# A hybrid encoder layer: block products for part of five input column groups, and one running account for the background work

## The chip, the cores and the metric

The kernel runs on one core of a Trainium2 chip. The metric is the device time of one execution in microseconds (us), the median of several runs. A profiled execution of the same program gives the trace from which all durations below are taken. Engines are named as in the profile: PE multiplies matrices, DVE (vector) and ACT (scalar) do elementwise work, SP issues the DMA transfers. Each engine works through its own instructions in the order in which the program issued them, and waits there for data or for a free buffer.

## The reference

One layer, with 256 positions and 4096 channels, in float32:

```python
xn = rms_norm(x, norm_g[l])
h = jnp.einsum('bsd,de->bse', xn, w_in[l])                # 4096 -> 14336 columns
c_val, c_glu, c_gate, q, k, v, a_gate = jnp.split(h, split_pts, axis=-1)

conv_out = conformer_conv(c_val, c_glu, conv_w[l], ...)   # GLU, depthwise conv of 31 taps,
conv_out = conv_out * jax.nn.silu(c_gate)                 # LayerNorm over channels, swish

q = rms_norm(q.reshape(B, S, ATTN_HEADS, HEAD_DIM), q_norm_g[l])
k = rms_norm(k.reshape(B, S, ATTN_HEADS, HEAD_DIM), k_norm_g[l])
attn = longnet_mixture(q, k, v, rel_bias)                 # 16 heads of 128
attn_out = attn * jax.nn.silu(a_gate)

mixed = jnp.concatenate([conv_out, attn_out], axis=-1)
x = x + jnp.einsum('bse,ed->bsd', mixed, w_out[l])        # 4096 -> 4096
```

The LayerNorm takes its mean and variance over all 2048 convolution channels, so nothing behind it can begin before the last channel is convolved.

## The kernel before

**Matrix products.** To keep float32 precision, every operand is split in two parts, a rounded high part and the rest (`wh`, `wl` for weights, `xh`, `xl` for rows of x), and each product is three matmuls: high by high, low by high, high by low. A matmul takes 128 channels of the contraction, 128 positions and 512 columns. The contraction of 4096 is 32 slices `k`, or 16 pairs of slices; one DMA of 1 MB brings the weights of a pair, 1024 columns wide (`load_pair`). A slice costs 12 matmuls: two halves `e` of the columns, two halves `s` of the positions, three each.

**Groups.** The columns are worked through in 18 groups of 1024 (`GROUPS`): groups 0 to 3 `conv` (value and GLU gate of 512 channels each), then four times `agv` (attention gate and v of four heads) and `qk` (query and key of the same heads), that is 4 to 11, then 12 and 13 `gate` (gates of the convolution), and 14 to 17 `out`. The main loop (from L905 on) issues, for each slice n of the 14 input groups, its first half's high matmuls, the rest of the slice before, the split of the weights three slices ahead (`split_w`, L199: ACT makes `wh`, DVE makes `wl`; eight slots), its first half's low matmuls, and then calls `pump`. At the end of a group `evacuate` (L610) moves the sums out of PSUM, with the factor `rstd` of the normalization of x, which the operands don't hold yet (x is multiplied by `norm_g` alone), and starts the background work that they make possible.

**Background work** is written as generators that issue a few instructions and yield their cost, a pair (DVE ns, ACT ns). `glu_post`, `ag_post` and `gate_post` transpose a tile of 512 channels to channels by positions (`turn`, L299: two DVE transpositions of 32x32 blocks, then four steps of four ACT copies). `conv_gen` (L326) applies the 31 taps to 16 chunks of 128 channels, one DVE instruction a tap and chunk. `ln_gen` (L378) is the LayerNorm. `qk_norm` (L428) normalizes and turns the queries and keys of four heads, `head_gen` (L459) is the attention of one head, with four matmuls of its own. `mix_split_gen` (L528) splits the finished rows for the output groups.

**Lanes.** The generators stand in lanes. `pump` (L588), called once per slice, first fills two accounts, DVE's and ACT's, by a quota (`STEP`, 950 and 1400; in the gate groups `GATE_STEP`, 1300 and 1600) but not above the quota, and then lets the lanes step in a fixed order: the gate lane, the foreground lane `fg` (transpositions, norms and heads in the order in which they came; the first three take one step each), twice the mix lane, and up to eight times the convolution lane. A step takes its cost from the accounts, and no generator steps while one of the two is at or below zero:

```python
        for gen in list(self.gens)[: self.width]:
            if min(left) <= 0:
                break
```

**The output groups** are issued by the class `Out` (L672). Ten of the 16 pairs are plain. Six, the pairs 0 to 5 of attention rows (`FUSED`), are taken as a two by two block product with seven instead of eight block multiplications (21 matmuls instead of 24), which needs sums of blocks of the rows (`mix_fuse`) and of the weights (`split_fused`, L722), four more PSUM banks (`m1`, `m5`, `m6`, `m7`) and further additions at the end (`add_more`, L874). The eight PSUM banks are two sets of four, `acc` and `side`; heads and the LayerNorm use `side`. Weights are split ahead whenever the slots allow it. `OUT_ORDERS` says in which order the pairs come: pairs 8 to 15 are convolution rows, 0 to 7 attention rows, and the first output group begins with 8, 9, 10. Before a pair the code loops until its rows have been issued:

```python
            for k in (2 * j, 2 * j + 1):
                while k not in mh:
                    pump()
```

Of the kernel before, what the change touches and what calls it, by code (L numbers as in the profile page):

```python
# [50 lines left out]
FUSED = (0, 1, 2, 3, 4, 5)  # L51
OUT_ORDERS = [(8, 9, 10, 0, 6, 1, 11, 2, 7, 3, 12, 4, 13, 5, 14, 15)]
OUT_ORDERS += 3 * [(8, 9, 0, 10, 1, 11, 2, 6, 3, 7, 4, 12, 5, 13, 14, 15)]
# [29 lines left out]
class Lane:  # L83
# [9 lines left out]
    def step(self, left):  # L93

        spent = 0
        for gen in list(self.gens)[: self.width]:
            if min(left) <= 0:
                break
            try:
                cost = next(gen) or 0  # L100
            except StopIteration:
                self.gens.remove(gen)
                continue
            cost = cost if isinstance(cost, tuple) else (cost, 0)
            for i in range(2):
                left[i] -= cost[i]
            spent += sum(cost)
        return spent
# [3 lines left out]
def layer_kernel(  # L112
# [17 lines left out]
    def t4(name):  # L130
        return sb.tile([P, 4, 256], F32, tag="c4", bufs=15, name=name)
# [13 lines left out]
    def rsqrt(src, shape, mul, eps, name):  # L145
# [6 lines left out]
        cost = 60 + n  # L152
# [24 lines left out]

    raw_tiles = {}

    def load_pair(j, cuts=(0, 2048), between=None):  # L180

        g, jj = divmod(j, n_pairs)
        if g >= NG:
            return
        if groups[g][0] == "out":
            jj = (OUT_ORDERS[g - n_in][jj] + n_pairs // 2) % n_pairs
# [7 lines left out]
    w_split = {}  # L194

    def ws(name):
        return sb.tile([P, 1024], F32R, tag="ws", bufs=W_SLOTS, name=name)

    def split_w(n):  # L199
        j, kk = divmod(n, 2)  # L200
        src = raw_tiles[j][:, kk]
        wh, wl = ws(f"wh{n}"), ws(f"wl{n}")
        if n:
            nc.scalar.copy(wh, src)  # L204
            nc.vector.tensor_sub(wl, src, wh.bitcast(F32))  # L205
        else:
            a, b = slice(0, 512), slice(512, 1024)
            nc.vector.tensor_copy(wh[:, a], src[:, a])
            split_x(0)
            nc.scalar.copy(wh[:, b], src[:, b])  # L210
            for c in (a, b):
                nc.vector.tensor_sub(wl[:, c], src[:, c], wh[:, c].bitcast(F32))
        w_split[n] = (wh, wl)
        if kk == 1:
            del raw_tiles[j]
            load_pair(j + RAW)

    xh, xl = {}, {}
# [30 lines left out]
    def split_x(k):  # L249
# [6 lines left out]
        xh[k], xl[k] = h, l  # L256

    state = {}

    def finish_rstd():  # L260
# [5 lines left out]
        state["rstd"] = [keep[:, s : s + 1] for s in range(2)]  # L266

# [31 lines left out]
    def turn(tile_, name, flip=False):  # L299
# [6 lines left out]
        for s in range(2):  # L306
            nc.vector.transpose(flat[:, 512 * s : 512 * s + 512], src[:, 512 * s : 512 * s + 512])
            yield 620
        blocks = flat.rearrange("p (s t b x) -> p s t b x", s=2, t=4, b=4)
        dst = src.rearrange("p (t s a x) -> p s t a x", t=4, s=2, a=4)  # L310
        for b in range(4):
# [6 lines left out]
            yield 0, 1240  # L318
# [7 lines left out]
    def conv_gen(cb):  # L326
# [4 lines left out]
        for tp in range(0, 4, 2):  # L331
            for t in (tp, tp + 1):
# [5 lines left out]
                yield 335  # L338
            for k in range(TAPS):
# [4 lines left out]
                for t in (tp, tp + 1):  # L344
# [5 lines left out]
                    yield 335  # L350
# [4 lines left out]
    def channel_mean(srcs, name):  # L355

        tot = sb.tile([P, S], F32, tag="rs_big", bufs=6, name=name + "tot")
        for i, make in enumerate(srcs):
# [6 lines left out]
            yield 1135  # L365
            if i:
                nc.vector.tensor_add(tot, tot, part)
                yield 335
# [9 lines left out]
    def ln_gen():  # L378
# [4 lines left out]
        for cb in range(4):  # L383
            nc.vector.tensor_sub(cT[cb], cT[cb], bcast4(mu))
            yield 1135

        def square(cb):
            sq = t4(f"sq{cb}")
            nc.scalar.activation(sq, cT[cb], AF.Square)
# [4 lines left out]
        for cb in range(4):  # L394
            nc.vector.tensor_mul(cT[cb], cT[cb], bcast4(r))
            yield 1135
        for cb in range(4):
            for t in range(4):
# [5 lines left out]
                if t % 2 == 1:  # L404
                    yield 900
# [4 lines left out]
    def gate_post(cb, g):  # L410
# [4 lines left out]
        for t in range(4):  # L415
            nc.vector.tensor_mul(cT[cb][:, t, :], cT[cb][:, t, :], g[:, t, :])
            mix_ready[NH + 4 * cb + t] = cT[cb][:, t, :]
            yield 335
# [9 lines left out]
    def qk_norm(hg):  # L428
        st = sb.tile([P, 16], F32, tag="rs_small", bufs=6, name=f"ssqk{hg}")
        both = (qt[hg], kt[hg])  # L430
        for i, src in enumerate(both):
            sq = t4(f"sq{hg}_{i}")
            nc.scalar.activation(sq, src, AF.Square)
            yield 0, 1000
            yield
            for s in range(2):
# [5 lines left out]
                yield 600  # L442
        r = yield from rsqrt(st, [P, 16], 1.0 / DH, NORM_EPS, f"rqk{hg}")
        for i, src in enumerate(both):
            for s in range(2):
# [5 lines left out]
                yield 600  # L451
# [4 lines left out]
        yield 650  # L456
        qk_ready[hg] = True

    def head_gen(hg, hh):  # L459
        h = 4 * hg + hh  # L460
        hs = slice(DH * hh, DH * hh + DH)
        while hg not in qk_ready:
# [24 lines left out]
        yield 1200  # L487
# [5 lines left out]
        yield 0, 700  # L493
# [3 lines left out]
        yield 600  # L497
        tmp = t2(f"turn_p{h}")
        nc.vector.transpose(tmp, pr)  # L499
        yield 620  # L500
        blocks = tmp.rearrange("p (i j b x) -> p j i b x", i=2, j=2, b=4)
        dst = pr.rearrange("p (j i a x) -> p j i a x", j=2, i=2, a=4)
        for b in range(4):
# [5 lines left out]
            yield 0, 800  # L509
# [11 lines left out]
        yield 400  # L521
# [6 lines left out]
    def mix_split_gen():  # L528
        waiting, done = list(OUT_ORDERS[0]), 0
        while waiting:  # L530
# [10 lines left out]
            if j in FUSED:  # L541
                yield from mix_fuse(j)
                continue
            for kk in (2 * j, 2 * j + 1):
# [5 lines left out]
                yield 335  # L550

    def mix_fuse(j):


        a0, a1 = mix_ready[2 * j], mix_ready[2 * j + 1]
        a11, a21, a12, a22 = a0[:, :P], a0[:, P:], a1[:, :P], a1[:, P:]
        sums = t2(f"mix_sums{j}")
        s1, s2, s3, s4 = (sums[:, P * i : P * i + P] for i in range(4))
        nc.vector.tensor_add(s1, a21, a22)
        nc.vector.tensor_sub(s2, s1, a11)  # L560
        yield 400
        nc.vector.tensor_sub(s3, a11, a21)
        nc.vector.tensor_sub(s4, a12, s2)
        yield 400
        b0, b1 = new_split(2 * j, "m"), new_split(2 * j + 1, "m")
        more = sb.tile([P, 2, 512], F32R, tag="c4", bufs=15, name=f"mx{j}")
        parts = [[b[:, :P] for b in b0], [b[:, P:] for b in b0], b1]
        parts.append([more[:, i, : 3 * P] for i in range(2)])
        for (h, l), src in zip(parts, (a11, s1, a1, sums[:, P:])):
            nc.scalar.copy(h, src)  # L570
            nc.vector.tensor_sub(l, src, h.bitcast(F32))
            yield 300, 300
        names = {"a11": parts[0], "s1": parts[1]}
        names["a12"] = [b[:, :P] for b in b1]
        names["a22"] = [b[:, P:] for b in b1]
        for i in range(3):
            names[f"s{i + 2}"] = [more[:, hl, P * i : P * i + P] for hl in range(2)]
        mx[j] = names
# [7 lines left out]
    left = [0, 0]  # L586

    def pump():  # L588

        for i, quota in enumerate(GATE_STEP if progress["in"] >= 0 else STEP):  # L590
# [417 lines left out]
```

## Time and profile before

| | us |
|---|---|
| median of the three runs | 1602.81 |
| lowest and highest run | 1602.33, 1603.76 |
| the profiled execution | 1603.12 |
| span of its trace, first to last instruction | 1601.3 |
| PE busy in the span | 1590.5 |
| DVE busy | 1195.0 |
| ACT busy | 968.2 |

The mean granted clock of PE is 0.998 of full speed. In the rows below a line of the groups view reads: source line, engine, operation, result and operands, shapes, count; then busy time, mean duration of one in ns; then the idle time of the engine before them and what ended it. A line of the view of one source line gives the shortest, median and longest duration in ns and the start of the first and last in us. Lines of the views in time begin with start and duration. A busy share of PE alone does not say that it works at its peak; the distance from one matmul's start to the next does.

### The profile page before, as it was taken

Reading aid. Unit: us, or ns where it says so; the run is one execution under the profiler, and the core shown is the slowest. Engines: PE = TensorE matmul, PEld = TensorE weight load, DVE = VectorE, ACT = ScalarE, POOL = GpSimd, SP = SyncE. Lnnn points to the kernel's source line nnn. Section 1 sums busy time; section 2 is a strip of 40 time slices with the busy share of each in tenths; the row PEclk is TensorE's granted clock in tenths of the full one; section 3 lists DMA queues with packets and bytes.
Section 4 is the critical chain, followed back from the end, with each engine's and each line's share of the span. In section 5 each row is a group of like instructions: output and inputs, shape, how many; then the busy total and the mean of one; then the engine's idle time right before and its main releaser. Section 6 shows DMA issues by size and latency. Waiting matters only on the chain.

```text
span 1601.3 us, 18984 instructions
## 1 busy us (share of the span) xinstructions
PE 1590.5 (99%) x6986; PEld 1312.8 (82%) x6986; DVE 1195.0 (75%) x1630; ACT 968.2 (60%) x1480; POOL 0.2 (0%) x4
## 2 busy tenths in 40 slices
PE   9999999999999999999999999999999999999999
PEld 7888888888888888888888888888878877888887
DVE  6668888888888887678755556555467889888886
ACT  6763534445453467755779557754789865545453
POOL 0000000000000000000000000000000000000000
PEclk9999999999999999999999999999999999999999
DMA  9755555555555555555555555455545556665653
GB/s 377 289 184 198 196 186 201 192 184 207 188 190 204 184 195 191 186 186 191 179 195 189 192 203 190 173 187 207 194 163 190 184 210 232 232 229 215 248 198 143
DMA packets 52892, 323.53 MB, mean 202 GB/s; under 512 B 5792, under 2 KB 8480, under 8 KB 16192
## 3 DMA queue, kind: packets, MB, share of 16 engines
q1 hardware_dynamic: 52512, 322.05, 56.4%
q8 instruction: 54, 0.88, 0.2%
q10 hardware_dynamic: 288, 0.28, 0.1%
q14 instruction: 38, 0.31, 0.1%
HBM read 318.08 MB, written 4.23 MB: 201 GB/s over the span
## 4 chain that ended last, share of the span: by engine, by line
PE 96%; ACT 1%; DVE 1%; issue 0%; DMA 0%; DVEq 0%; ACTq 0%
PE acc L662 25%; PE acc L663 25%; PE acc L665 25%; PE c L784 5%; PE c L782 5%; PE c L783 5%; PE m L784 1%; PE m L782 1%; PE m L783 1%; PE po L514 1%; PE psc L475 1%; ACT gate L315 0%; ACT pr L505 0%; DMA first_x<-in_x_cols_dram 0%; DVE t24l L736 0%
## 5 line engine op out<-in xcount | busy, mean ns | idle before, releaser
L205 DVE TENSOR_TENSOR wl<-raw,wh 128x1024 fp32r<-128x1024 f32 x447 | 546.9, 1224 | 336.9 <-ACT wh L204 335.9
L204 ACT CAST wh<-raw 128x1024 fp32r<-128x1024 f32 x447 | 469.6, 1052 | 434.9 <-PE acc L663 241.5
L662 PE MATMUL acc<-wh,xh 128*128 128x512 f32 x1792 | 703.8, 393 | 1.3 <-ACT xh L252 1.3
L663 PE MATMUL acc<-wh,xl 128*128 128x512 f32 x1792 | 698.4, 390 | 0.0
L665 PE MATMUL acc<-wl,xh 128*128 128x512 f32 x1792 | 483.7, 389 | 0.0
L662 PEld LDWEIGHTS acc<-wh,xh 128*128 128x128 f32 x1792 | 337.0, 188 | 72.3 <-ACT xh L252 1.6
L663 PEld LDWEIGHTS acc<-wh,xl 128*128 128x128 f32 x1792 | 336.8, 188 | 70.1 <-DVE xl L253 0.2
L665 PEld LDWEIGHTS acc<-wl,xh 128*128 128x128 f32 x1792 | 336.3, 188 | 70.3
L346 DVE SCALAR_TENSOR_TENSOR cT<-conv,wT,cT 128x241 f32<-128x241 f32 (+14 forms) x480 | 201.6, 471 | 0.0
L782 PE MATMUL c<-oh,mh 128*128 128x512 f32 x320 | 125.3, 391 | 0.5 <-ACT oh L716 0.5
L784 PE MATMUL c<-ol,mh 128*128 128x512 f32 x320 | 125.1, 391 | 0.5 <-DVE ol L717 0.5
L783 PE MATMUL c<-oh,ml 128*128 128x512 f32 x320 | 125.0, 391 | 0.0
L716 ACT CAST oh<-raw 128x1024 fp32r<-128x1024 f32 x80 | 83.2, 1051 | 50.8 <-PE c L783 34.4
L717 DVE TENSOR_TENSOR ol<-raw,oh 128x1024 fp32r<-128x1024 f32 x80 | 96.1, 1222 | 21.8 <-ACT oh L716 15.2
L505 ACT COPY pr<-turn_p 32x128 f32<-32x128 f32 x256 | 75.9, 297 | 9.2 <-DVE turn_p L499 5.7
L782 PEld LDWEIGHTS c<-oh,mh 128*128 128x128 f32 x320 | 60.5, 189 | 13.5 <-ACT oh L716 1.0
L784 PEld LDWEIGHTS c<-ol,mh 128*128 128x128 f32 x320 | 60.3, 189 | 13.5 <-DVE ol L717 1.0
L783 PEld LDWEIGHTS c<-oh,ml 128*128 128x128 f32 x320 | 60.5, 189 | 12.8
L732 ACT CAST t24h<-t 128x1024 fp32r<-128x1024 f32 x24 | 25.2, 1051 | 40.3 <-PE c L783 24.1
L736 DVE TENSOR_TENSOR t24l<-t,t24h 128x1024 fp32r<-128x1024 f32 x24 | 29.4, 1226 | 17.3 <-ACT t24h L732 17.3
L732 ACT CAST t13h<-t 128x1024 fp32r<-128x1024 f32 x24 | 25.3, 1053 | 18.2 <-DVE t L748 14.2
L732 ACT CAST bh<-raw 128x1024 fp32r<-128x1024 f32 x24 | 25.3, 1053 | 16.3 <-PE m L783 16.3
(195 smaller groups left out, 1030.8 us busy)
## 6 DMA issues: line engine op xcount, KB each, us to landing
raw<-in_w_dram SPq DMA_DIRECT2D x286, 1024.0 KB, 4.8
x<-in_x_dram SPq DMA_DIRECT2D x8, 512.0 KB, 7.4
xr<-in_x_dram SPq DMA_DIRECT2D x8, 512.0 KB, 6.0
out_dram<-xr SPq DMA_DIRECT2D x15, 256.0 KB, 2.9
xT<-in_x_cols_dram SPq DMA_DIRECT2D x7, 512.0 KB, 6.9
T<-bias_dram SPq DMA_DIRECT2D x16, 192.0 KB, 5.0
raw<-in_w_dram SPq DMA_DIRECT2D x3, 512.0 KB, 6.2
raw<-in_w_dram SPq DMA_DIRECT2D x2, 256.0 KB, 4.4
```

What stands on the lines that cost most here:

```text
L204: nc.scalar.copy(wh, src)
L205: nc.vector.tensor_sub(wl, src, wh.bitcast(F32))
L346: nc.vector.scalar_tensor_tensor(c[:, t, lo:hi], a[:, t, lo + sh : hi + sh], wT[:, ch, k : k + 1], c[:, t, lo:hi], op0=ALU.mult, op1=ALU.add,)
L505: nc.scalar.copy(dst[32 * b : 32 * b + 32, :, :, 3 - a, :], backwards(blocks[32 * a : 32 * a + 32, :, :, b, :]),)
L662: nc.tensor.matmul(a, hs, wp, start=k == 0, stop=False)
L663: nc.tensor.matmul(a, ls, wp, start=False, stop=False)
L665: nc.tensor.matmul(a, hs, wp, start=False, stop=k == KT - 1)
L716: nc.scalar.copy(h, src)
L717: nc.vector.tensor_sub(l, src, h.bitcast(F32))
L782: nc.tensor.matmul(acc, a[0], b[0], start=start, stop=False)
L783: nc.tensor.matmul(acc, a[1], b[0], start=False, stop=False)
L784: nc.tensor.matmul(acc, a[0], b[1], start=False, stop=stop)
```

## The change

1. **Block products in the input.** Groups 2 to 6 (the third to the seventh) take pairs 2, 4, 6 and 8 as seven block products, the other twelve as before. They are issued by the class that was `Out`, now `Stream`, which also splits the weights of all groups. These groups use both sets of PSUM banks, so heads wait for group 7 (`state["side"]`).
2. **Normalized x.** Block sums mix positions, so `rstd` can't be applied at the end: during group 1 x is loaded a second time, multiplied by `norm_g` and `rstd` (laid out along the positions by way of DRAM) and split again (`split_xn`); the sums of the four pairs are made there too. From group 2 on `evacuate` has no factor.
3. **The account.** The quotas are gone. Every matmul that is issued credits both accounts with a share of its time (`FILL`), up to `SAVED`; splits, evacuations and background steps all spend from them, at costs that are set anew.
4. **Others.** The first output group has four block pairs, not six; the block sums use other signs, are made in place in the weights' buffer, and the rows of block pairs are also split as plain ones; the residual x is loaded two pairs earlier; the big tiles (`c4`) have 18 buffers instead of 15, for which a DMA scratch area is cut to 2048 bytes; 11 instead of 7 warm-up matmuls.

```diff
-STEP, GATE_STEP = (950, 1400), (1300, 1600)
-AHEAD = 3
+PRODUCT = 227
+FILL, SAVED = (0.93, 0.93), (1300, 1600)
 RAW = 3
+C4 = 18
...
+FUSED_IN = range(2, 7)
+FUSED = [(2, 4, 6, 8) if g in FUSED_IN else () for g in range(N_IN)] + [range(4)] + 3 * [range(6)]
+ORDERS = N_IN * [range(16)]
+ORDERS += [(8, 9, 10, 0, 6, 1, 11, 2, 7, 3, 12, 4, 13, 5, 14, 15)]
...
+    left = [0, 0]
+
+    def spend(dve, act=0):
+        left[0] -= dve
+        left[1] -= act
+
+    def credit(ns):
+        for i in range(2):
+            left[i] = min(left[i] + FILL[i] * ns, SAVED[i])
...
+    def split_xn(k):
+        src = xT[k]
+        nc.vector.scalar_tensor_tensor(
+            src, src, g_cols[:, k : k + 1], state["rstd_row"], op0=ALU.mult, op1=ALU.mult
+        )
+        h, l = new_split(k, "n")
+        nc.scalar.copy(h, src)
+        nc.vector.tensor_sub(l, src, h.bitcast(F32))
+        xh[k], xl[k] = h, l
+        spend(900, 400)
...
     def turn(tile_, name, flip=False):
...
-            yield 620
+            yield 700
...
-            yield 0, 1240
+            yield 0, 1610
...
     def conv_gen(cb):
...
-                    yield 335
+                    yield 470
...
     def head_gen(hg, hh):
...
-        while hg not in qk_ready:
+        while hg not in qk_ready or not state["side"]:
             yield
...
-        yield 1200
+        yield 1370
...
-        yield 0, 700
+        yield 0, 1380
...
-        yield 600
+        yield 860
...
-        yield 620
+        yield 700
...
-            yield 0, 800
+            yield 0, 1190
...
-    def pump():
-        for i, quota in enumerate(GATE_STEP if progress["in"] >= 0 else STEP):
-            left[i] = min(left[i] + quota, quota)
-        gate_lane.step(left)
-        fg.step(left)
+    def pump(more=0):
+        credit(more)
+        gate_lane.step(left, spend)
+        fg.step(left, spend)
         for _ in range(2):
-            mix_lane.step(left)
+            mix_lane.step(left, spend)
         for _ in range(8):
-            if not conv_lane.step(left):
+            if not conv_lane.step(left, spend):
                 break
...
     def products(n, e, part):
...
+        credit(PRODUCT * (4 - 2 * part))
...
     class Stream:
...
             def part(k):
...
                 nc.scalar.copy(h, src)
                 nc.vector.tensor_sub(l, src, h.bitcast(F32))
+                spend(1225, 1055)
...
             def three():
                 r = blocks()
                 hl = halves("b22s", "b22")
                 nc.scalar.copy(hl[:, 0, :], r[:, 3, :])
+                nc.vector.tensor_add(r[:, 0, :], r[:, 0, :], r[:, 3, :])
+                nc.vector.tensor_add(r[:, 1, :], r[:, 0, :], r[:, 2, :])
+                nc.vector.tensor_sub(hl[:, 1, :], r[:, 3, :], hl[:, 0, :].bitcast(F32))
+                spend(2050, 620)
...
         def triple(self, acc, a, b, start, stop):
...
+            credit(3 * PRODUCT)
...
                 for k in (2 * j, 2 * j + 1):
+                    while k not in rows[0]:
+                        pump(PRODUCT)
...
-    for _ in range(7):
+    for _ in range(11):
         nc.tensor.matmul(spin[:, :P], ones, ones, start=True, stop=True)
...
+    for g in range(n_in):
+        if FUSED[g]:
+            stream.group(g)
+            continue
+        if g > FUSED_IN[-1]:
+            state["side"] = True
+        for k in range(KT):
...
                 products(n, 0, 0)
                 if k == KT - 1:
                     products(n, 0, 1)
                 if k > 0 and n > 1:
                     products(n - 1, 1, 0)
                     products(n - 1, 1, 1)
                 if n + 3 < KT:
                     split_x(n + 3)
+                stream.step()
                 if k < KT - 1:
                     products(n, 0, 1)
...
+            if g == FUSED_IN[0] - 1:
+                if k % 4 == 0:
+                    load_xT(k, 4, nc.sync)
+                if k >= 2:
+                    split_xn(k - 2)
...
             pump()
```

More of the change, by code (lines that the diff above doesn't have):

```diff
@@ L192, in load_pair @@
                 between()
[L194 to L218, printed above, removed]
+    xh, xl, xsum = {}, {}, {}
     def new_split(k, nm):
@@ L832, in fused @@
             )
-            for i, (acc, an, bn, freed) in enumerate(rows):
+            for i, (acc, an, bn, freed) in enumerate(order):
                 self.before()
@@ L840, in fused, with plain @@
                     pump()
[L842 to L858 removed]
+        def plain(self, u, j, rows, one, first):
             for k in range(2):
@@ L948, in layer_kernel @@
     progress["in"] = KT + 2
-    out.run()
+    for g in range(n_in, NG):
+        stream.group(g)
 def _layout(i):
```

455 lines of the change are left out of this document (254 added, 201 removed).

## The prediction

> **What bounds the kernel now.** I read the page's first part, the waits of PE, the groups of instructions, and then single rows in time.
>
> ```profile
> span 1601.3 us, 18984 instructions
> PE 1590.5 (99%) x6986; PEld 1312.8 (82%) x6986; DVE 1195.0 (75%) x1630; ACT 968.2 (60%) x1480; POOL 0.2 (0%) x4
> ...
> 9.29 0.93 PE acc L665 x4
> 13.40 0.91 PE acc L665 x4
> 16.12 0.91 PE acc L665 x4
> ...
> PE m L782 <- ACT t24h L732: 1.2, 1, 1.2
> PE m L784 <- DVE t24l L736: 1.1, 3, 0.5
> ```
>
> The matmul stream sets the time. One slice k (12 matmuls) takes 16.12 - 13.40 = 2.72 us, 0.2267 us a matmul, and PE hardly waits: the two waits shown are the longest that the 24 block-product pairs of the output groups cause (some 3 us over all of them). So matmuls removed count in full, as long as DVE and ACT deliver what PE reads, and that includes the background work: convolution, LayerNorm, attention, gates. When is it done today?
>
> ```profile
> L346 DVE SCALAR_TENSOR_TENSOR cT<-conv,wT,cT x480: 430/471/482, 114.4 to 697.4; 128x242 f32<-128x242 f32 x16, 128x245 f32<-128x245 f32 x16, 128x248 f32<-128x248 f32 x16, 128x251 f32<-128x251 f32 x16
> L400 ACT ACTIVATE cT<-cT,vec_cols x16: 584/595/610, 800.8 to 868.3; 128x256 f32<-128x256 f32 x16
> L519 DVE TENSOR_TENSOR agv<-agv,po x16: 382/414/417, 648.0 to 1245.0; 128x256 f32<-128x256 f32 x16
> L782 PE MATMUL c<-oh,mh x320: 387/389/628, 1257.8 to 1596.5; 128*128 128x512 f32 x160
> ```
>
> Convolution taps end at 697 us, LayerNorm at 868, the last head at 1245; the output groups begin at 1257.8. The heads end 13 us before they are needed; the convolution has long been done.
>
> **The change, part by part.**
>
> *Matmuls.* A plain pair is 24 matmuls, seven block products are 21. Groups 2 to 6 get 4 such pairs each: 5 x 4 x 3 = 60 fewer. The first output group goes from six to four: 6 more. Net -54 x 0.2267 = **-12.2 us**.
>
> *Start.* Eleven warm-up matmuls instead of seven.
>
> ```profile
> 1.04 3.36 PE L900 MATMUL spin<-ones 128*128 128x128 f32 x14 [1.04 <-DVE ones L143]
> 5.73 0.80 PE L662 MATMUL acc<-wh,xh 128*128 128x512 f32 x1 [1.33 <-ACT xh L252]
> 6.85 0.63 PE L662 MATMUL acc<-wh,xh 128*128 128x512 f32 x1
> 7.70 0.63 PE L662 MATMUL acc<-wh,xh 128*128 128x512 f32 x1
> ...
> 9.26 1.05 ACT L204 CAST wh<-raw 128x1024 fp32r<-128x1024 f32 x1 [0.47 <-DMA raw<-in_w_dram]
> 11.42 0.39 PE L662 MATMUL acc<-wh,xh 128*128 128x512 f32 x1
> ```
>
> Seven end at 4.40, so 0.48 us each; eleven would end at 6.3, 0.6 us late. In return the first eight real matmuls, 0.42 us apart (two in 7.70 - 6.85), might run at 0.23: at most 8 x 0.2 = 1.6 us back, of which the copy of the third weight slice, ready near 10.3 us where PE used it at 11.4, lets 1.1 through. Between +0.6 and -1.1 I take **-0.5**. The Trainium skill ("TensorE: Matmul & The Clock Gate", section "Part 1: The HAM clock gate") says that the array runs at half rate until a window of about 3.4 us was busy; by that rule a gapless row of warm-up matmuls gives the whole -1.1, and a long idle stretch later costs the slow start again.
>
> *Splitting a block pair.*
>
> ```profile
> L736 DVE TENSOR_TENSOR bl<-raw,bh 128x1024 fp32r<-128x1024 f32 x24 | 29.3, 1221 | 0.5 <-ACT bh L732 0.2
> L748 DVE TENSOR_TENSOR t<-raw 128x1024 f32<-128x1024 f32 x24 | 29.2, 1219 | 0.0
> L759 DVE TENSOR_TENSOR t<-raw,t 128x512 f32<-128x512 f32 x24 | 16.4, 684 | 0.0
> L205 DVE TENSOR_TENSOR wl<-raw,wh 128x1024 fp32r<-128x1024 f32 x447 | 546.9, 1224 | 336.9 <-ACT wh L204 335.9
> L204 ACT CAST wh<-raw 128x1024 fp32r<-128x1024 f32 x447 | 469.6, 1052 | 434.9 <-PE acc L663 241.5 <-DVE cT L346 173.1 <-issue 6.4
> ```
>
> DVE works 4 x 1.22 + 3 x 0.684 = 6.93 us per block pair against 2.45 for a plain one, while PE needs 21 x 0.2267 = 4.76. Pairs 2, 4, 6, 8 alternate with plain ones: 9.4 us of DVE per 10.2 of PE, which the eight weight slots bridge. The output groups alternate likewise with some 3 us lost over 24 pairs; for 20 pairs with background among them I take **+3** (0 to 40, the upper end if every excess of 2.2 us showed). The split of normalized x (32 x 0.9 us of DVE), the second load of x (8 x 512 KB) and the round trip of rstd lie in group 1, whose DVE then carries 1.22 + 0.9 of each 2.72 us: nothing, or a few us if the row of rstd comes late (bound 5). In groups 7 to 13 the stream keeps one weight slice fewer ahead, as group 6 leaves four slots filled and each iteration adds just one: **+2** for seven group ends (0 to 7).
>
> *The account.* Here lies the change's weight. Each matmul now credits both accounts 0.93 x 227 = 211 ns, capped at 1300 (DVE) and 1600 (ACT); a split costs 1225 and 1055; the lanes step only while **both** are above zero. Follow one iteration of a plain group: ten matmuls (+2110) reach the cap from any debt above -810, the split takes it to 75 (ACT 545), the last two matmuls add 422: at `pump` there are **497 for DVE and 967 for ACT**, no more. Against that:
>
> - a transposition copy step costs 1610 ACT, a head's 1190 or 1380, its DVE steps 1370, 860, 700; each alone ends the pump, and the convolution, last in line, gets nothing;
> - with nothing ahead of it, the convolution gets two taps (497, 27, -443). Before, a quota of 950 at 335 a tap gave three, beside an ACT step of 1240 out of 1400.
>
> Groups 7 to 13 have 7 x 32 = 224 pumps. The foreground lane asks one pump per such step: 16 heads x 8 = 128; query and key norms 25 each (2 squares, 4 sums, 2 of the root, 4 products, 12 for two transpositions, 1), three of them 75 and 18 left of the first; three gate transpositions of 6, 18: 239 in all. It does not fit; the convolution gets crumbs. In group 1 the split of x takes 900 of the 497: no background at all. In groups 2 to 6 the account closes at 24 x 1307 (plain k) - 4 x 2519 (block pairs) - 5.5 to 7 (evacuation) = some 15 us a group, 75 in all, of which the ACT debts of five transpositions (20 pumps of about 1.1) lose 22.
>
> Carried through all pumps by these rules: of 496 tap steps (480 taps and 16 starts) **120 are dealt before the output groups** (86 in groups 2 to 6, 34 after), with 4 heads and two transpositions left as well. To test the bookkeeping I carried the old quotas through the old code the same way: last tap in iteration 251, LayerNorm's end 312, last head 443. At 2.72 us from 6.5 us on, plus 2 us of PE for each head so far (4, 7, 16), that is 697, 869 and 1244; the rows above show 697.4, 868.3 and 1245.0.
>
> *What PE then waits for.* The first output group starts with pair 8, whose rows need LayerNorm and a gate, and the code pumps until they exist.
>
> ```profile
> L315 ACT COPY qk<-turn_q 32x256 f32<-32x256 f32 x64 | 25.8, 404 | 0.9
> L505 ACT COPY pr<-turn_p 32x128 f32<-32x128 f32 x256 | 75.9, 297 | 9.2 <-DVE turn_p L499 5.7
> L489 ACT ACTIVATE pr<-pr,nm 128x256 f32<-128x256 f32 x32 | 16.0, 501 | 0.6 <-DVE nm L486 0.4
> 116.30 1.23 DVE L346 SCALAR_TENSOR_TENSOR cT<-conv,wT,cT 128x241 f32<-128x241 f32 x3
> L364 DVE TENSOR_REDUCE mup<-cT 128x256 f32<-128x1024 f32 x3 | 6.0, 2012 | 0.0
> L384 DVE TENSOR_TENSOR cT<-cT,mu 128x1024 f32<-128x1024 f32 x4 | 4.9, 1217 | 0.0
> 1201.02 1.13 PE po L514 x4
> 1202.15 0.86 PE psc L475 x4
> ```
>
> 1. Attention first: two transpositions, 32 x 0.404 = 12.9; four heads at 16 x 0.297 + 2 x 0.50 + 0.4 = 6.1 of ACT, 24.5; about 8 of DVE and PE between: 45 us.
> 2. Then 376 tap steps back to back. Three take 1.23 us, so (1.23 - 0.47) / 2 = 0.38 apart: 143 us (176 if each took its whole 0.47).
> 3. LayerNorm: 8 x 2.01 + 8 x 1.22 + six additions of 0.41 + 4 for the root = 32; squares, means, table loads, Silu and gate about 9 more: 41 us.
>
> Together **+229**. Gates 1 to 3 are turned one after the other behind it (1.4 DVE + 6.5 ACT + 2 each) and pairs 10, 12 and 14 wait for parts of them: **+19** (5 to 30). The four late heads leave the stream, 4 x (1.13 + 0.86) = **-8**. A slow start after the idle time, as the eight first matmuls show: **+2**.
>
> Sum: 1601.3 - 12.2 - 0.5 + 3 + 2 + 229 + 19 - 8 + 2 = **1835.6 us**. The profiled execution took 1603.1 in all, the median of the runs is 1602.8: 1.5 us beside the span. Forecast **1837 us**.
>
> **The rivals.**
>
> *Faster: the background is done in time.* Then 1601.3 - 12.2 - 0.5 + 3 + 2 + 1.5 = **1595**, or 1590 without the small losses. For it: DVE has room as a whole, 1195 us busy plus 20 x 4.5 for the pairs, 29 for x and some 25 for evacuation (7 or 8 additions of 0.68 in each of five groups) is 1340, 84% of the span. It holds if the cap does not bind at the pump; by the order of the statements it does. Chance 0.10.
>
> *The account binds only on DVE* (ACT debt somehow harmless): 124 of 263 us of convolution and LayerNorm would be dealt and no head left, so 230 taps, 88 us, + 41 instead of 229, and no -8: **1745**. The code asks for the lower of the two accounts. Chance 0.03.
>
> *Block pairs starve PE as well*: the excess of 2.2 us shows at 20 pairs, +40 on top: **1878**. Against it the output groups' row. Chance 0.05.
>
> **How the numbers follow.** 0.82 for the forecast. Its own doubts: taps at 0.47 (+32), attention less serial (-20), late gates (-14, +11), small terms (-5, +10). The range 1795 to 1885 holds nearly all of that and the third rival, about 0.83. A difference under 0.2% (3.2 us) cannot be told from none: faster 0.10, same 0.01, slower 0.89.
>
> **What would show it.** PE idle for one stretch of some 229 us beginning near 1240 us (1257.8 - 13.6 - 8 + 4), ended by ACT's copy of the first gated rows, with DVE nearly full of taps in it; first tap near 245 us, not 114; about 120 taps before the stretch; PE records down by 54 plus the extra warm-up's 8. If taps end before 1240, or PE's waits there are below 50 us, the account was read wrongly and the first rival holds.

## The result, and the profile after

| | before | after |
|---|---|---|
| median, us | 1603.01 (1602.33 to 1603.76, 4 runs) | 1893.18 (1889.82 to 1895.25, 4 runs) |
| ratio, 95% interval | | 1.1808 (1.1788 to 1.1828) |
| the profiled execution, its span | 1603.12, 1601.3 | 1889.82, 1887.9 |

The changed kernel is slower by 18%. That is 56 us above the forecast of 1837 and 8 us above the upper end of its range. From the first part of the page the busy times, with three rows of the span in 40 slices of 47 us (each digit is a share in tenths; PEclk is the clock that PE was granted):

```profile
PE 1609.6 (85%) x6940; PEld 1310.3 (69%) x6940; DVE 1334.3 (71%) x1834; ACT 996.3 (53%) x1546; POOL 0.2 (0%) x4
...
PE   9999999999999999999999999973000176999999
...
DVE  6657778787888655565556555553999866688887
...
PEclk9999999999999999999999999985555588999999
```

PE has 6986 - 54 + 8 = 6940 records, as counted. It stands still in one stretch, in which DVE is first nearly full and PE's granted clock falls to half. DVE's busy time of 1334 us is what the first rival had added up (1340). So DVE has room as a whole and is loaded at the wrong time.

When is the background work done now? The same lines of the code as before, in the view of one line (shortest, median and longest duration in ns, then the start of the first and the last in us):

```profile
L388 DVE SCALAR_TENSOR_TENSOR cT<-conv,wT,cT x480: 427/473/490, 273.2 to 1470.4; 128x242 f32<-128x242 f32 x16, 128x245 f32<-128x245 f32 x16, 128x248 f32<-128x248 f32 x16, 128x251 f32<-128x251 f32 x16
L443 ACT ACTIVATE cT<-cT,vec_cols x16: 584/586/602, 1502.7 to 1519.4; 128x256 f32<-128x256 f32 x16
L557 PE MATMUL po<-pr,agv x64: 377/378/796, 707.9 to 1319.6; 128*128 128x256 f32 x64
L830 PE MATMUL c<-wh,nh x480: 387/389/796, 194.5 to 630.7; 128*128 128x512 f32 x160
L711 PE MATMUL acc<-wh,nh x896: 387/389/580, 631.4 to 1261.2; 128*128 128x512 f32 x180
L830 PE MATMUL c<-wh,mh x336: 387/389/796, 1507.1 to 1883.4; 128*128 128x512 f32 x168
```

The last tap has moved from 697 to 1470 us, the LayerNorm's last step from 868 to 1519, the last head from 1245 to 1320. The last three rows give the stages: groups 2 to 6 from 194.5 (`nh` there are the rows of normalized x), groups 7 to 13 from 631.4, the output groups from 1507.1 us. How many taps ran in each stretch? The windows view of line L388 alone (start and end, length, busy time of DVE with the number of taps, granted clock, share and rate of the DMA engines):

```profile
273.00:631.00 358.00, 34.58 (x82) 1.00 0.54 196
631.00:1262.00 631.00, 14.72 (x34) 1.00 0.53 190
1262.00:1321.00 59.00, 0.00 (x0) 0.55 0.10 31
1321.00:1471.00 150.00, 141.66 (x364) 0.50 0.00 0
```

Before the output groups 82 + 34 = 116 taps were dealt; with the four starts of the chunks begun that is the 120 steps of the prediction. The other 364 run in one stretch while PE stands still. The waits of PE (total us, times, longest):

```profile
PE mupm L414 <- DVE mutot L409: 159.3, 1, 159.3
PE c L830 <- ACT mh L587: 40.3, 4, 15.3
PE psc L518 <- DVE qk L498: 21.5, 1, 21.5
PE po L557 <- ACT pr L548: 21.3, 4, 7.2
PE vapm L414 <- DVE vatot L409: 13.8, 1, 13.8
PE m L832 <- DVE t24l L797: 7.5, 18, 0.4
PE acc L711 <- ACT wh L766: 5.2, 6, 2.8
```

The first, third, fourth and fifth row lie in the stretch from 1262 to 1507 us: the LayerNorm's mean waits for the taps (159.3), the heads for their rows, the variance for its sums. Of the second row, one wait of 11.4 us ends that stretch (the first gated rows); the other three, 28.9 us, are the late gates. The last two rows are the supply of split weights, which the prediction had put at little.

### The profile page after: what moved, and what is told of

It is laid out like the page before. It is cut to its first block, busy times and chain, and to the rows that moved or that the text cites. A ratio compares the mean times of both kernels' runs of the same rounds, so it can differ in the third digit from the quotient of the medians.

```text
span 1887.9 us, 19245 instructions
## 1 busy us (share of the span) xinstructions
PE 1609.6 (85%) x6940; PEld 1310.3 (69%) x6940; DVE 1334.3 (71%) x1834; ACT 996.3 (53%) x1546; POOL 0.2 (0%) x4
## 4 chain that ended last, share of the span: by engine, by line
PE 67%; DVE 22%; ACT 8%; issue 2%; DMA 1%; SPq 0%; ACTq 0%; DVEq 0%
PE acc L711 12%; PE acc L712 12%; PE acc L714 12%; PE c L830 9%; PE c L831 9%; PE c L832 8%; DVE cT L388 7%; DVE wl L767 4%; ACT wh L766 2%; DVE raw L805 1%; DVE t13l L797 1%; DVE bl L797 1%; PE m L832 1%; ACT t13h L796 1%; ACT t24h L796 1%
## 5 line engine op out<-in xcount | busy, mean ns | idle before, releaser
L711 PE MATMUL acc<-wh,nh 128*128 128x512 f32 x896 | 352.2, 393 | 0.0
L712 PE MATMUL acc<-wh,nl 128*128 128x512 f32 x896 | 348.8, 389 | 0.0
L714 PE MATMUL acc<-wl,nh 128*128 128x512 f32 x896 | 241.8, 389 | 0.0
L714 PEld LDWEIGHTS acc<-wl,nh 128*128 128x128 f32 x896 | 168.2, 188 | 35.2
L711 PEld LDWEIGHTS acc<-wh,nh 128*128 128x128 f32 x896 | 168.2, 188 | 34.9
L712 PEld LDWEIGHTS acc<-wh,nl 128*128 128x128 f32 x896 | 168.2, 188 | 34.9
L388 DVE SCALAR_TENSOR_TENSOR cT<-conv,wT,cT 128x241 f32<-128x241 f32 (+14 forms) x480 | 191.0, 473 | 0.0
L830 PE MATMUL c<-wh,nh 128*128 128x512 f32 x480 | 188.0, 392 | 3.4 <-ACT wh L766 3.4
L832 PE MATMUL c<-wl,nh 128*128 128x512 f32 x480 | 188.0, 392 | 0.6 <-DVE wl L767 0.5
L831 PE MATMUL c<-wh,nl 128*128 128x512 f32 x480 | 187.7, 391 | 0.0
L830 PE MATMUL c<-wh,mh 128*128 128x512 f32 x336 | 134.5, 400 | 40.3 <-ACT mh L587 40.3
L414 PE MATMUL mupm<-mutot,ones 128*128 128x256 f32 x2 | 1.2, 714 | 159.3 <-DVE mutot L409 159.3
L711 PE MATMUL acc<-wh,xh 128*128 128x512 f32 x256 | 103.4, 404 | 5.7 <-ACT wh L766 5.2
```

The lines of the kernel that those rows point to most:

```text
L388: nc.vector.scalar_tensor_tensor(c[:, t, lo:hi], a[:, t, lo + sh : hi + sh], wT[:, ch, k : k + 1], c[:, t, lo:hi], op0=ALU.mult, op1=ALU.add,)
L711: nc.tensor.matmul(a, hs, wp, start=k == 0, stop=False)
L712: nc.tensor.matmul(a, ls, wp, start=False, stop=False)
L714: nc.tensor.matmul(a, hs, wp, start=False, stop=k == KT - 1)
L830: nc.tensor.matmul(acc, a[0], b[0], start=start, stop=False)
L831: nc.tensor.matmul(acc, a[1], b[0], start=False, stop=False)
```

## The experiments

The theory on trial is the prediction's: the ceiling of the account starves the convolution. Its rivals are that the block pairs fill DVE, and that the account's second condition (ACT's debt) does it alone. Besides, 52 us of the span were unexplained: 1887.9 against a sum of 1835.6. Runs without an interval are single executions.

### The ceiling twice as high

```diff
-FILL, SAVED = (0.93, 0.93), (1300, 1600)
+FILL, SAVED = (0.93, 0.93), (2600, 3200)
```

> One line: the ceiling of the account is doubled, 2600 and 3200 instead of 1300 and 1600. If the ceiling starves the convolution, the bookkeeping has 198 of 263 us of convolution and LayerNorm dealt before the output groups, and every head: 72 tap steps are left, 28 us, and LayerNorm, 37 us. The one long wait of PE falls from 245 to about 65 us, the heads' 8 us come back into the stream: about 1721 us. Rival (DVE has no room beside the block pairs, so what is dealt earlier is paid for in the groups): about 1890 us, with PE waits in groups 2 to 13 instead.

Measured: 1719.14 us, 2 below the expectation. With the same credit per matmul, only a higher ceiling, 174 us of the median are gone. The same row of PE's waits in this kernel:

```profile
PE mupm L414 <- DVE mutot L409: 40.8, 1, 40.8
```

So the ceiling of the account takes most of the time, as predicted. The expectation came from the same bookkeeping as the 120 steps.

### The account asks for DVE alone

```diff
-            if min(left) <= 0:
+            if left[0] <= 0:
```

> The changed kernel, but the lanes stop only when DVE's account is at or below zero; ACT's is not asked. The bookkeeping has 136 of 263 us dealt and every head: 205 tap steps (79 us) and LayerNorm (37) in the long wait, 116 instead of 245 us, 8 us of heads back in the stream: about 1772 us. So the two conditions would share the blame, half each. Rival (the ceiling alone matters, ACT's debt is harmless): about 1890 us; or ACT, no longer held back, is late with its weight copies: PE waits for them in groups 7 to 13.

Measured: 1771.49 us, 122 us less than the change as it is. The condition on the lower of the two accounts is worth some four tenths of the slowdown: a step of 1610 ns of ACT stops the taps, which need no ACT. The long wait is some 124 us here (from 1269 to 1392.7), about half of the 245; that the ceiling causes what is left is argued from the bookkeeping, which said 116. The prediction's second rival had 1745 for this rule; its sum lacks what group 1 and the block pairs cost. (The gain of this edit and that of the higher ceiling don't add up: a step that is dealt by one rule is not there for the other.)

### No block pairs in the input groups

```diff
-FUSED = [(2, 4, 6, 8) if g in FUSED_IN else () for g in range(N_IN)] + [range(4)] + 3 * [range(6)]
+FUSED = N_IN * [()] + [range(4)] + 3 * [range(6)]
```

> Groups 2 to 6 take all 16 pairs as plain pairs, 60 matmuls more; the account and the second split of x stay. If the account is the cause, the long wait stays: the bookkeeping has 106 of 263 us dealt, 269 tap steps (104 us), LayerNorm (37) and some 52 of attention are left, 193 us instead of 245, and 13.6 us more of matmuls: about 1852 us. Rival (the block pairs take DVE's time and that is what starves the convolution): the long wait goes, about 1640 us.

Measured: 1836.3 us, 16 below the expectation. PE has 60 matmuls more to do (13.6 us), and the wait remains:

```profile
PE mupm L414 <- DVE mutot L409: 121.2, 1, 121.2
```

If DVE's work for the block pairs had pushed out the taps, this wait would be gone. It shrinks by 38 us, which fits the account too: the splits of these pairs no longer spend from it. Group 13 ends only 3.6 us later in spite of the 60 matmuls, so some 10 us of waits ahead of it went with the block pairs; that is one reason why the time lies below the expectation, and it points at their splitting.

### Full credit and a high ceiling

```diff
-FILL, SAVED = (0.93, 0.93), (1300, 1600)
+FILL, SAVED = (1.0, 1.0), (4000, 5000)
```

> The account is credited with the whole matmul time (1.0 instead of 0.93) and its ceiling is 4000 and 5000. By the bookkeeping the last tap is dealt in iteration 373 of 448, LayerNorm ends in 410, the last head in 445, and no pump is called in a wait. The long wait (245 us) and the waits for gates (some 36 us with the slow start) go, 8 us of heads come back: about 1615 us. Rival (no room on DVE): PE waits for split weights in the groups, 1700 us or more.

Measured: 1643.89 us, 29 above the expectation. The long wait is gone: the taps end at 1067.6 us, the heads are done in time, and the output groups begin at 1290.5. But the kernel doesn't reach the 1595 of the first rival, so something else costs 49 us. The first waits of PE in this kernel:

```profile
PE acc L711 <- ACT wh L766: 13.6, 12, 5.1
PE m L832 <- DVE t24l L797: 11.1, 24, 0.6
```

Both point at the supply of split weights. Two places show in the trace: group 1, and the splitting of block pairs.

### Group 1: a chain across two engines

In the changed kernel the windows view of all engines (PE, PEld, DVE, ACT and POOL, busy time and number each; then granted clock and DMA) shows in group 1:

```profile
100.00:120.00 20.00, 17.23 (x70) 13.90 (x69) 8.28 (x12) 5.59 (x9) 0.00 (x0) 0.91 0.69 248
120.00:140.00 20.00, 19.45 (x80) 14.37 (x79) 15.16 (x26) 9.04 (x14) 0.00 (x0) 1.00 0.56 204
```

Instead of 20 / 0.2267 = 88 matmuls only 70 and 80 are done in 20 us, though neither DVE nor ACT is full. The chain of waits (start, duration, what) says why:

```profile
89.33 7.51 DMA rstd_dram<-rstd
...
98.23 11.12 DMA xT<-in_x_cols_dram
...
112.50 0.41 DVE xT L254
...
113.24 1.05 ACT wh L766
...
114.31 1.23 DVE wl L767
115.54 0.41 DVE xT L254
```

The first tile of x stands in SP's queue behind the round trip of `rstd`, 7.5 us for writing 256 numbers, and takes 11.1 us itself. Then each slice is a chain: DVE multiplies x, ACT's copy of the product must wait for it, ACT's copy of the next weights stands behind that copy, and DVE's `wl` waits for these weights before DVE can multiply the next x. From one product to the next it takes 115.54 - 112.50 = 3.04 us; PE needs 2.72 a slice. Neither DVE nor ACT is overloaded; the order makes them take turns.

The edit multiplies x one slice before it is split, and loads the tiles earlier (the first at the end of group 0):

```diff
+            if n in (24, 26):
+                load_xT(2 * n - 48, 4, nc.sync)
             if g == FUSED_IN[0] - 1:
-                if k % 4 == 0:
-                    load_xT(k, 4, nc.sync)
-                if k >= 2:
-                    split_xn(k - 2)
+                if k % 4 == 0 and k < 24:
+                    load_xT(k + 8, 4, nc.sync)
+                for _ in range(2 if k >= 4 else 0):
+                    if scaled[0] < min(k, KT):
+                        scale_xn(scaled[0])
+                        scaled[0] += 1
+                for _ in range(2 if k >= 4 else 0):
+                    if halved[0] < min(k - 1, scaled[0] - 1):
+                        split_xn(halved[0])
+                        halved[0] += 1
```

> In group 1 x is multiplied by its factors one slice ahead of its split (so ACT's copy no longer waits for DVE within the same slice), starting with slice 4 and catching up by two a slice, and its tiles are loaded two steps earlier. If the 27 us that groups 0 to 6 took beyond the forecast come from DVE and ACT waiting for each other in turn (3.05 us a slice against PE's 2.72) and from the late first tile, about 20 us go: 1873 us. Rival (the loss is the round trip of the factors through DRAM): the first slices wait as before, 1885 us or more.

Measured: 1867.18 us (1866.36 to 1869.27), ratio 1.165 (1.163 to 1.1669). The same two windows, and the stages:

```profile
100.00:120.00 20.00, 20.00 (x90) 16.54 (x89) 14.62 (x24) 9.91 (x15) 0.00 (x0) 1.00 0.87 311
120.00:140.00 20.00, 20.00 (x90) 16.58 (x89) 18.65 (x36) 11.11 (x17) 0.00 (x0) 1.00 0.76 272
```
```profile
L835 PE MATMUL c<-wh,nh x480: 389/389/397, 180.5 to 610.1; 128*128 128x512 f32 x160
L716 PE MATMUL acc<-wh,nh x896: 387/389/580, 610.8 to 1240.5; 128*128 128x512 f32 x180
```

Group 2 begins at 180.5 instead of 194.5, and groups 2 to 6 take 610.8 - 180.5 = 430.3 us instead of 436.9. The same instructions in another order are worth 26.0 us of the median and 22.5 of the span (1887.9 to 1865.4). The edit changes two things, the order of the steps and the time of the loads, and no run separates them. The windows help: between 105 and 115 us, where the first tile is awaited, the changed kernel has 26 matmuls and this one 46, some 4.5 us of the 14.0 by which group 2 begins earlier; the other 9.5 lie in the slices behind, where only the chain is left.

> The fuller account (credit 1.0, ceiling 4000 and 5000: 1644 us by itself) together with x multiplied one slice ahead (-26 us by itself). The account decides when background is dealt, the other edit how group 1 runs: about 1618 us if the two are independent. Rival: with more background dealt in groups 1 and 2 the order of x's steps hides less or more, 1605 or 1630 us.

Together with full credit: 1619.99 us, against 1643.89 without the new order; groups 2 to 6 take 436.7 us (183.5 to 620.2). The first waits of PE here are still those of the block pairs, 11.3 us in 25 waits for `t24l`.

### Block pairs: sums in place

The new code makes the block sums in the weights' own buffer. So the first sum can only be made behind the split of the weights that it overwrites (`b`); ACT's copy of it (`t13h`) begins only then, and DVE has to wait for that copy before it makes `t13l`. (The second sum, in the same buffer, must in turn wait until both have read the first.) The wait of DVE in the changed kernel:

```profile
DVE t13l L797 <- ACT t13h L796: 48.2, 41, 1.5
```

The edit gives both sums tiles of their own, and makes the first ahead of the split of `b`, so that ACT finds it ready (tiles and order change together):

```diff
             def one():
                 r = blocks()
+                kept["t13"] = pairs("t13s")
+                nc.vector.tensor_add(kept["t13"], r[:, 0:2, :], r[:, 1:4:2, :])
                 both("b", r[:, 0:3:2, :], ("b11", "b21"))
-                nc.vector.tensor_add(r[:, 0:2, :], r[:, 0:2, :], r[:, 1:4:2, :])
...
-                nc.vector.tensor_add(r[:, 0, :], r[:, 0, :], r[:, 3, :])
-                nc.vector.tensor_add(r[:, 1, :], r[:, 0, :], r[:, 2, :])
+                t24 = kept["t24"] = pairs("t24s")
+                nc.vector.tensor_add(t24[:, 0, :], kept["t13"][:, 0, :], r[:, 3, :])
+                nc.vector.tensor_add(t24[:, 1, :], t24[:, 0, :], r[:, 2, :])
```

> The changed kernel with nothing but the block sums of the weights in tiles of their own, made before the first split. The long wait stays. With x multiplied one slice ahead groups 2 to 6 took 430.3 us against 421.7 of matmuls; if that is ACT's copy waiting for the sum in place, about 8 us go there and some 5 in the output groups: about 1880 us. Rival: with so little background dealt the chain is hidden, 1890 us or more.

Measured, with this edit alone: 1873.36 us (1872.78 to 1874.46), ratio 1.1689 (1.1673 to 1.1705), 7 below the expectation. Groups 2 to 6 take 428.4 us (193.4 to 621.8; 436.9 without the edit), the time from the output groups' start to the end is 373.5 instead of 380.8, and DVE's wait for `t13h` is not among its larger ones any more.

> As 'both', and the block sums of the weights are made in tiles of their own, before the first split, as the kernel before did it, instead of in place behind it. In place, ACT's copy of the first sums can't start until DVE has finished the split of the unsummed blocks and the sum, and DVE then waits for that copy, some 1.06 us a block pair. Groups 2 to 6 take 22 us more than their matmuls in the kernel with the fuller account, the output groups 7 us. If that is this chain, some 12 to 20 us go: about 1603 us. Rival (DVE's total load in these groups): no change beyond 4 us.

All three edits (full credit, new order in group 1, own tiles): 1595.68 us in one execution, some 7 under the expectation. The same kernel in five executions:

> The same kernel as 'both_fresh', timed: 1596 us, faster than the kernel before by 0.4%, with an interval that leaves out no difference. Rival: the one look was lucky, within 0.2% of before.

Measured: 1596.09 us (1595.59 to 1597.11, 5 runs) against 1603.13 of the kernel before, ratio 0.9959 (0.9947 to 0.9972). This version is 0.4% faster than the kernel before, a small difference, but clear of its interval. Its stages and its largest wait of PE:

```profile
L844 PE MATMUL c<-wh,nh x480: 388/389/395, 183.7 to 605.1; 128*128 128x512 f32 x160
L716 PE MATMUL acc<-wh,nh x896: 386/389/585, 605.8 to 1252.0; 128*128 128x512 f32 x180
L844 PE MATMUL c<-wh,mh x336: 387/389/628, 1252.9 to 1590.1; 128*128 128x512 f32 x168
```
```profile
PE acc L716 <- ACT wh L771: 7.3, 8, 1.7
```

Groups 2 to 6 take 605.8 - 183.7 = 422.1 us; five times 372 matmuls at 0.2267 are 421.7. In these groups the block pairs now come without loss, 14.6 us less than with the sums in place (436.7). The kernel as a whole keeps 7.0 of the 13.3 us that fewer matmuls and the shorter start save (12.2 + 1.1, see the table below): group 2 begins at 183.7 where 179.5 had been reckoned, and PE still waits for copies of weights.

### More credit still

To see whether the last wait can go, DVE's credit was set above the time that passes, under a lower ceiling:

```diff
-FILL, SAVED = (1.0, 1.0), (4000, 5000)
+FILL, SAVED = (1.1, 1.0), (2600, 3200)
```

> As 'both_fresh', with credit 1.1 for DVE and 1.0 for ACT and the ceiling at 2600 and 3200: less may be saved up, so fewer splits stand behind a heap of background steps. The bookkeeping has the last tap in iteration 318 instead of 373, LayerNorm's end in 364 instead of 410, and again no pump in a wait. PE's waits for weight copies, 7.2 us, should fall to some 3: about 1592 us. Rival: the larger credit fills groups 2 to 6 too far, 1600 us.

Measured: 1599.93 us (1599.46 to 1600.79, 10 runs), ratio 0.9982 (0.9972 to 0.9991); the rival's number, not the theory's. The wait for `wh` falls from 7.3 to 3.9 us, but group 7 begins at 610.4 instead of 605.8: most of the time moved to groups 2 to 6. Which of the two numbers did it was not separated; full credit with the higher ceiling stays the best version run.

### The late gates two at a time

```diff
-    fg, gate_lane, mix_lane, conv_lane = Lane(3), Lane(1), Lane(1), Lane(1)
+    fg, gate_lane, mix_lane, conv_lane = Lane(3), Lane(2), Lane(1), Lane(1)
```

> The changed kernel with a gate lane of two instead of one, so that the next gate is turned while the one before waits for LayerNorm. If the time behind the long wait (36 us more than the output groups' own) is the gates turned one after the other, pair 10 no longer waits and some 20 us go: about 1873 us. Rival (DVE's backlog of block sums and the half clock after the wait): 1885 us or more.

Measured: 1885.54 us; the theory (1873) missed. PE's waits on `mh` do fall:

```profile
PE c L830 <- ACT mh L587: 29.4, 3, 11.4
```

That is 29.4 instead of 40.3 us, and the output groups take 369.1 us instead of 380.8. (In both kernels 11.4 us of this row end the long wait; behind it two waits of 17.9 us are left of three with 28.9.) But the output groups begin at 1514.7 instead of 1507.1: group 13 ends 1.6 us later, and the long wait, in which a second gate is now turned, is 6 us longer. Of 11.7 us gained, 7.6 are paid ahead.

## Where the prediction was right, and the steps that failed

The direction, the mechanism, the place of the wait and the count of the dealt steps were right; the sum was 52 us short, so that the time lies above the range. The terms against what the trace of the changed kernel shows (span, us):

| term | predicted | measured | from |
|---|---|---|---|
| matmuls | -12.2 | -12.2 | 54 records fewer; their price is not measured by itself |
| start | -0.5 | -1.1 | third slice at 10.31 instead of 11.42 |
| group 1 | 0 (bound 5) | +21.6 | 15.0 + 6.6: group 2 begins at 194.5, not 6.5 + 64 x 2.72 - 1.1 = 179.5; and 436.9 - 430.3 in groups 2 to 6, against the run with the new order |
| block pairs | +3 | +8.6 | 430.3 - 421.7, without the disturbance of group 1 |
| group ends, heads in 7 to 13 | +2 - 8 | -10.3 | 1262.2 - 631.4 - 224 x 2.72 = 21.5 for twelve heads, where sixteen at 1.13 + 0.86 make 31.8 |
| long wait | +229 | +245 | 1262 to 1507 |
| late gates, slow clock | +19 + 2 | +36 | 380.8 against 343.5 + 1.4 |

These make 1601.3 + 287.6 = 1888.9; the span is 1887.9.

**The account: right.** 120 steps before the output groups as counted; the first tap stands at 273 instead of 245, and at 252 in the run that takes group 1's waits away. Doubling the ceiling, dropping the account's second condition and taking the block pairs away moved the wait as the theory said. What follows from the code's arithmetic alone came out as counted.

**Group 1: the step that failed.** The prediction had put "1.22 + 0.9 of each 2.72 us" on DVE and therefore "nothing, or a few us if the row of rstd comes late (bound 5)". Each engine's sum does fit. What was left out is the order in which DVE and ACT wait for each other, 3.04 us a slice in place of 2.72. The term is 21.6 us, more than four times its bound, and the run with the new order and earlier loads takes 22.5 us of span off. The late row of `rstd` was named and its bound about held: some 4.5 us belong to the first tile.

**Block pairs: the same omission, smaller.** The +3 came from the output groups of before, whose sums have tiles of their own. The in-place sums were in the diff, but not costed as a wait. The +40 of the third rival did not come. With own tiles the loss in groups 2 to 6 is nil, and the output groups of the best version take 341.7 us to the end, less than the 344.9 that the old ones would.

**The long wait: mis-sized by 16 us.** The taps took 150 us instead of 143 (the fourth row of their windows), and the LayerNorm 36 instead of 41 (from the end of the taps at 1470.9 to 1507.1). Attention took 59 instead of 45. One of its two transpositions in the view in time of ACT (in brackets the idle time before, and what ended it), then the first head in the chain of waits:

```profile
1266.06 6.60 ACT L357 COPY qk<-turn_q 32x256 f32<-32x256 f32 x16 [2.34 <-DVE turn_q L349]
```
```profile
1283.75 2.06 PE psc L518 x4
...
1296.07 2.09 PE po L557 x4
```

From the end of group 13 at 1262.0 to the first head's matmuls it takes 21.7 us. The prediction had counted the copies of the two transpositions, 12.9 us; they took 13.2, but DVE's steps ahead of, between and behind them also stand in the way. That is 8.8 of the 14 us. The four heads then took 37.3 us instead of 32.5. Here PE is slower: four matmuls take 2.06 and 2.09 us, not 0.86 and 1.13, at a granted clock of 0.55 (the third row of the windows). Four such pieces lie in the chain, one `psc` and three `po`, 1.2 + 3 x 0.96 = 4.1 us; how much of this is the clock alone is not shown.

**Behind the wait: mis-sized by 15 us.** The waits of PE from 1510 us on, and one of the transpositions behind them in the view in time of ACT:

```profile
PE c L830 <- ACT mh L587: 28.9, 3, 15.3
PE m L832 <- DVE t24l L797: 3.5, 8, 0.4
```
```profile
1521.76 6.60 ACT L357 COPY gate<-turn_g 32x256 f32<-32x256 f32 x16 [1.79 <-DVE turn_g L349]
```

Three waits for late gates make 28.9 of the 36 us, so the bound of 30 held for them alone, but not the +19. Ahead of the transposition shown DVE splits and sums a block pair (1518.02 to 1520.51 us), 2.5 us that are not in the prediction's 1.4 + 6.5 + 2 for a gate; what makes the longest wait, 15.3 us, stays open. The waits for `t24l` are 3.5 us more; the rest, some 4 us, fits the slow stretches behind the waits, but is not measured by itself. With own tiles the output groups get 7.3 us of the 36 back.

**The start** gained more than taken:

```profile
1.04 4.59 PE L971 MATMUL spin<-ones 128*128 128x128 f32 x22 [1.04 <-DVE ones L147]
...
6.33 0.40 PE L711 MATMUL acc<-wh,xh 128*128 128x512 f32 x1
6.57 0.40 PE L712 MATMUL acc<-wh,xl 128*128 128x512 f32 x1
...
10.31 0.50 PE L711 MATMUL acc<-wh,xh 128*128 128x512 f32 x1
```

The 22 records stand without a gap and end at 5.63 us, not at the 6.3 that 0.48 us for each of eleven had given, and from 6.33 us on the matmuls are 0.24 us apart. The rule of the Trainium skill ("TensorE: Matmul & The Clock Gate", "Part 1: The HAM clock gate") by which this gives -1.1 agrees with this trace.

**The range** ended at 1885 because the bounds of the small terms were taken one by one, and group 1, the block pairs, attention and the late gates all came out dearer together. Group 1 and the block pairs rest on one assumption, that engines which are not full don't delay each other; the runs show that it failed in both. For attention and the late gates the same is read from the chain of waits and not shown by a run.

**The first rival** was not far: with an account that deals early enough, and the two chains taken apart, the change does give 1596 us, where the rival had said 1595. That the numbers meet is in part chance: group 2 begins 4.2 us later than the rival's sum had it, and the output groups take 3.2 us less.

## What to carry to other kernels

A quota that is refilled to a ceiling deals at most the ceiling at each call, whatever the mean rate is: follow one iteration with its numbers and count the calls, and ask what each kind of step blocks. Where two engines hand work to each other, add up the loop (here 3.04 us a slice, where no engine had more than 2.72 to do) beside each engine's busy time; multiplying one slice ahead or giving a sum its own tile breaks such a loop at no cost in instructions. A long wait costs more than its length, since the work inside it and just behind it runs at half clock (0.50 and 0.55 of full speed in the windows above).

## What the runs showed of the hardware

A wait of PE of some 3 us is followed by a slow stretch as long as itself or longer. In the changed kernel PE waits for 3.2 us at the start of group 2 (the view in time, then the chain of waits):

```profile
207.33 0.80 PE L830 MATMUL c<-wh,nh 128*128 128x512 f32 x1 [3.23 <-ACT wh L766]
```
```profile
212.79 0.43 PE c L832
213.22 0.28 PE m L830
213.50 0.23 PE m L831
```

From 207.33 to 213.2 us most matmuls are 0.43 us apart, then 0.23: twelve of them take 5.9 us where 2.7 would do, so a wait of 3.2 us costs some 3 more. The Trainium skill ("TensorE: Matmul & The Clock Gate", "Why this matters for your kernels") warns of idle gaps above about 3 us between bursts of matmuls. The trace agrees; the slow stretch is 5.9 us here and, at the start of the output groups (1507.10 to 1510.45), 3.4 us. A shorter wait, the one for the first tile in group 1, was already enough:

```profile
111.29 0.80 PE L711 MATMUL acc<-wh,xh 128*128 128x512 f32 x1 [2.77 <-ACT wh L766]
```

Behind it the matmuls are 0.43 us apart until 114.0. In the clock record of this trace the half clock lasts 3.41 us around this wait and 6.83 us around the one of 3.2 us, that is one and two steps of 3.41 us, and all changes of the clock in the trace lie whole numbers of such steps apart. So the price of a wait comes in steps, and 2.77 and 3.23 us of waiting, nearly the same, cost one step and two.

DVE's taps back to back overlap, also in the stretch where nothing else runs. The chain of waits:

```profile
1454.91 15.95 DVE cT L388 x41
```

41 taps in 15.95 us are 0.389 us each, while the median duration of one is 0.473. The 364 taps of the long wait would make 172 us as a sum over durations; the fourth row of the windows has DVE busy with them for 141.66 us.
